# Convolutions that end in SiLU, and decay blocks made early, in a hybrid gMLP / gated DeltaNet / cross-attention layer

## The chip, the cores and the metric

The kernel runs on one core of a Trainium2 chip. The metric is device time in microseconds (us). The engines are named as the profile names them: PE is TensorE (matrix products), PEld its weight loads, DVE is VectorE, ACT is ScalarE, POOL is GpSimd, SP is SyncE, which issues most of the DMAs. Each engine works through its own instructions strictly in order; between engines there are semaphores.

## The reference, cut to what matters

One layer over 1024 tokens of width 2048: a norm, one input projection, three groups of heads, a gate on each, one output projection, a residual and a last norm. What the change touches is group B, a gated delta rule with 8 heads of width 128, in float32:

```python
def causal_conv_silu(x, w):                     # q, k and v of every head
    y = sum(w[k] * xp[:, k:k + S] for k in range(4))
    return jax.nn.silu(y)

qkv = causal_conv_silu(concat(d_q, d_k, d_v), conv_w)
q = l2norm(q) * 128 ** -0.5;  k = l2norm(k)
g = -exp(a_log) * softplus(d_a + dt_bias)       # log decay, one per token and head
g_cum = cumsum(g)                               # within a chunk
decay = exp(where(tri, g_cum[:, None] - g_cum[None, :], -inf))
a = where(strict, (k * beta) @ k.T * decay, 0)  # to be inverted, with 1 on the diagonal
attn_intra = where(tri, q @ k.T * decay, 0)
q_g = q * exp(g_cum)[:, None]
```

Two things of these are exponentials of the gate alone: the block `decay`, of which every pair of a chunk and a head has one, and the row factor `exp(g_cum)`, by which q is multiplied. Neither depends on q, k or v.

## The kernel before, in words

**Work and stages.** The sequence is taken in two halves of 512 tokens (`hf`), a half in four blocks of 128 (`NT`), and the kernel's delta rule takes chunks of 128 tokens (the reference has 64; the result is the same). A head's q, k and v are held with the 128 channels on the partitions and 512 tokens along the row. All large products run in three passes of split operands (`triple`, lines 460 to 464): a raw tile is cast on ScalarE to a high part (`whi`, `ahi`) and the rest is subtracted on VectorE (`wlo`, `alo`); `split_to` (437) does both. So every product of the projections hangs on ScalarE and VectorE.

The stages, with the times at which the profile has them:
- To about 124 us: the memory's keys and values, the norm of the first half of x, small parameters.
- The first stage, to about 413 us. For each half: the gate columns and `decays` (782), then the convolutions and preparation (`front`, 1128) of the first four heads, in two pairs, then their values (`early_values`, 1151). Results go to DRAM (`late_d`, `gt_d`). Weight tiles of 128 x 512 go through five buffers. Between these, `next_job` runs the norm of the second half of x and sums of row blocks that later products need.
- From about 413 us: the input projection's other columns, in five passes (`blocks(0)` to `blocks(4)`), each a seven-product scheme (`seven`, 1276). Beside them run the inverses (`inverse`, 971), the levels and scans of the first four heads (`backs`), then, at about 620 to 868 us, `front` for the last four heads, both halves, whose convolution inputs come back from DRAM (`p_d`), and later their values (`values`, 1175) and scans.
- From about 1280 us: the attention and the output projection.

**A convolution** (`conv`, 879). The projection's result is copied into `xr` with a halo of three tokens, ScalarE multiplies by the last of four weights, VectorE adds the other three (901). The weights in `cw` (672) are half of the given ones, so the sum is y/2. Lines 903 to 905 then make SiLU out of it: ScalarE takes tanh into a tile of the ring `tn`, and one VectorE instruction computes (t + 1) * y/2. There are 48 convolutions: q, k and v, eight heads, two halves; 24 in the first stage, 16 of q and k at 620 to 868 us, 8 of v later.

**A head's preparation** (`qk`, 915). GpSimd issues a DMA that spreads the head's cumulative decay over all partitions (`E`, 927; two buffers); ScalarE takes Exp of it for the row factor (`vs`, 929); then GpSimd masks E above the diagonal (930) and ScalarE takes Exp of each of its four blocks with a bias (933). E is scaled, multiplied into k k and q k products (953, 954), and q is multiplied by the row factor (955).

**Tables of ScalarE.** Functions come in tables; a change of table is an instruction of its own, ACT_TABLE_LOAD. SiLU, Exp and the tanh-GELU lie in different ones. Tanh, copies and squares need no change from the Exp table.

**Order of the work.** The program is first collected as a list of operations. `Plan.issue` (225) then simulates the engines with a price for each operation, and at every moment hands an engine, of the operations that are ready, the one of the lowest rank (`rank`, given where the operation is written; 5 if nothing is said). On ScalarE an operation that needs another table than the last one counts 1.5 ranks more (`STAY`, 253), and a load is priced at 1500 ns. `TABLES` (69) tells which functions this concerns: Exp, SiLU and GELU. The order found is what each engine then executes, and does not change at run time. Weight splits have rank 2, main products 9.

Of the kernel before, what the change touches and what calls it, by code (L numbers as in the profile page):

```python
# [17 lines left out]
P = 128  # L18
# [4 lines left out]
HT = 512  # L23
# [272 lines left out]
def kernel(  # L296
# [32 lines left out]
    def C(shape, name, dt=F32):  # L329
        return sb.tile(list(shape), dt, name=name, tag=name)[:]  # L330

    def DT(shape, name, dt=F32):
        return dr.tile(list(shape), dt, name=name, tag=name)[:]
# [41 lines left out]
    def tok(ap):  # L375

        return ap.rearrange("p (t c) -> p t c", c=P)
# [291 lines left out]
    pt = dnr()  # L669
    PE.transpose(pt[:, 0:105], rows[0:105], ident[0:105, 0:105])  # L670
    cw = C([P, 96], "cw")
    V.tensor_scalar(cw, pt[:, 0:96], 0.5, None, op0=ALU.mult)
    col2 = C([P, 9], "col2")
    V.tensor_copy(col2, pt[:, 96:105])

# [88 lines left out]


    abt = C([P, NT, 2 * NH], "abt")
    gr = C([NT * NH, P], "gr")
    y2 = C([P, 2 * NT, 64], "y2")
    G.memset(y2, 0.0)
    steps = C([P, HT], "steps")  # L770
    r3, ww = ([steps[:, i * P : (i + 1) * P] for i in two] for two in ((0, 1), (2, 3)))
    scs = [C([P, 7, NT, NH], f"sc{hf}") for hf in range(2)]
    sct = C([P, 5, NT, NH], "sct")
    gcs = [DT([NT, NH, P], f"gcd{hf}") for hf in range(2)]
    scan_banks, work = dnr.bufs[0:2], over(dnr.bufs[2:4])

    def decay_mm(a, k):
# [4 lines left out]
    def decays(hf, a):  # L782

        NU = NT * NH
        ab = ring["tn"]()[0:32]
        with rank(1):
            S.copy(ab, a[0:32])
        sc = scs[hf]
        beta, gg, gc, egl, edk, ngb, w0 = (sc[:, i] for i in range(7))
        w1, w2, w3, w4, egc = (sct[:, i] for i in range(5))  # L790
        tp = tpb()
        for tt in range(NT):
            PE.transpose(tp[:, tt * 32 : tt * 32 + 32], ab[:, tt * P : (tt + 1) * P], ident[0:32, 0:32])
        tpv = tp[:, 0 : NT * 32].rearrange("p (t c) -> p t c", c=32)
        with rank(1):
            S.copy(abt, tpv[:, :, 0 : 2 * NH])
            V.tensor_tensor(out=abt, in0=abt, in1=tpv[:, :, 2 * NH :], op=ALU.add)
            S.activation(beta, abt[:, :, NH:], AF.Tanh, scale=0.5)
            V.tensor_scalar(beta, beta, 1.0, 0.5, op0=ALU.add, op1=ALU.mult)
            V.tensor_tensor(out=w0, in0=abt[:, :, 0:NH], in1=rep(dtb, NT), op=ALU.add)  # L800
            S.activation(w1, w0, AF.Abs)
            S.activation(w1, w1, AF.Exp, scale=-1.0)
            V.tensor_scalar(w2, w1, 2.0, None, op0=ALU.add)
            V.reciprocal(w2, w2)
            V.tensor_tensor(out=w2, in0=w1, in1=w2, op=ALU.mult)
            V.tensor_tensor(out=w3, in0=w2, in1=w2, op=ALU.mult)
            V.tensor_scalar(w4, w3, 1.0 / 15.0, None, op0=ALU.mult)
            for c in (13.0, 11.0, 9.0, 7.0, 5.0, 3.0):
                V.scalar_tensor_tensor(w4, w4, 1.0 / c, w3, op0=ALU.add, op1=ALU.mult)
            V.scalar_tensor_tensor(w4, w4, 1.0, w2, op0=ALU.add, op1=ALU.mult)  # L810
            V.tensor_scalar(w0, w0, 0.0, None, op0=ALU.max)
            V.scalar_tensor_tensor(w0, w4, 2.0, w0, op0=ALU.mult, op1=ALU.add)
            V.tensor_tensor(out=gg, in0=w0, in1=rep(nal, NT), op=ALU.mult)
            dp = tpb()
            ggf = gg.rearrange("p t h -> p (t h)")
            PE.matmul(dp[:, 0:NU], utri, ggf, start=True, stop=True)
            PE.matmul(dp[:, NU : 2 * NU], ones, ggf, start=True, stop=True)
            gcf = gc.rearrange("p t h -> p (t h)")
            V.tensor_copy(gcf, dp[:, 0:NU])
            S.activation(egl.rearrange("p t h -> p (t h)"), dp[:, NU : 2 * NU], AF.Exp)  # L820
            V.tensor_tensor(out=edk.rearrange("p t h -> p (t h)"), in0=dp[:, NU : 2 * NU], in1=gcf,
                            op=ALU.subtract)
            S.activation(edk, edk, AF.Exp)
            S.activation(egc, gc, AF.Exp)
            V.tensor_scalar(ngb, egc, -1.0, None, op0=ALU.mult)
            V.tensor_scalar(w0, gc, -1.0, None, op0=ALU.mult)
            tp = tpb()
            PE.transpose(tp[0:NU, 0:P], gcf, ident)
            V.tensor_copy(gr, tp[0:NU, 0:P])
            Q.dma_start(gcs[hf].rearrange("t h p -> (t h) p"), gr)  # L830


    todo = []

# [44 lines left out]
    def conv(which, h, hf, o, a=None):  # L879
        ct = which * NH + h  # L880
        xr = ring["xr"]()
        w = [cw[:, k * 24 + ct : k * 24 + ct + 1] for k in range(4)]
        if h < NJ:
            if a is None:
                last = (which, h, hf) == (2, NJ - 1, 1)
                a = project([column(which, h)], order=(1, 0, 2, 3) if last else range(KT // KP))[0]
            next_job()
            with rank(1):
                S.copy(xr[:, 0:3], halo[:, which * NJ + h])
                S.copy(xr[:, 3:], a)  # L890
                if hf == 0:
                    S.copy(halo[:, which * NJ + h], xr[:, HT:])
                S.activation(o, xr[:, 3:], AF.Copy, scale=w[3])
        else:
            if hf == 0:
                G.memset(xr[:, 0:3], 0.0)
                Q.dma_start(xr[:, 3:], p_d[which][h - NJ][:, 0:HT])
            else:
                Q.dma_start(xr, p_d[which][h - NJ][:, HT - 3 :])
            S.activation(o, xr[:, 3:], AF.Copy, scale=w[3])  # L900
        for k in range(3):
            V.scalar_tensor_tensor(o, xr[:, k : k + HT], w[k], o, op0=ALU.mult, op1=ALU.add)
        t = ring["tn"]()
        S.activation(t, o, AF.Tanh)
        V.scalar_tensor_tensor(o, t, 1.0, o, op0=ALU.add, op1=ALU.mult)

    def by_token(o, src, scale):
        for tt in range(NT):
# [5 lines left out]

    def qk(h, hf, q, k, hs, gt):

        beta, edk, ngc = (scs[hf][:, i] for i in (0, 4, 6))
        bank = over(scan_banks) if h >= NJ else tpb
        qt, kt = to_tokens((q, bank()), (k, bank()))
        sumsq(hs[:, 1], kt)  # L920
        V.tensor_scalar(hs[:, 1], hs[:, 1], EPS, None, op0=ALU.add)
        V.reciprocal(hs[:, 3], hs[:, 1])
        V.scalar_tensor_tensor(hs[:, 2], hs[:, 3], -1.0, beta[:, :, h], op0=ALU.mult, op1=ALU.mult)
        V.tensor_tensor(out=hs[:, 3], in0=hs[:, 2], in1=edk[:, :, h], op=ALU.mult)
        kd = tok(ring["kd"]())
        e = tok(ring["E"]())
        G.dma_start(e, gcs[hf][:, h].partition_broadcast(P))
        vs = tok(ring["vs"]())
        S.activation(vs, e, AF.Exp)
        G.affine_select(out=e, in_=e, compare_op=ALU.is_ge, fill=NEG, base=0,  # L930
                        pattern=[[0, NT], [1, P]], channel_multiplier=-1)
        for tt in range(NT):
            S.activation(e[:, tt], e[:, tt], AF.Exp, bias=ngc[:, tt, h : h + 1])
        by_token(e, e, hs[:, 2])
        sumsq(hs[:, 0], qt)
        V.tensor_scalar(hs[:, 0], hs[:, 0], P * EPS, P * EPS * EPS, op0=ALU.mult, op1=ALU.add)
        by_token(kd, kt, hs[:, 3])
        rsqrt_to(hs[:, 4], hs[:, 1])
        V.tensor_tensor(out=hs[:, 4], in0=hs[:, 4], in1=hs[:, 1], op=ALU.mult)

        ch, cl = (ring["inv"](F32R).rearrange("p (t s c) -> p t s c", s=2, c=P) for _ in range(2))
        for i, src in enumerate((k, q)):
            split_to(ch[:, :, i], cl[:, :, i], tok(src), V)
        ai = tok(ring["ai"]())
        for t2 in range(NT // 2):
            d = work()
            for j in range(2):
                tt = 2 * t2 + j
                triple(d[:, j * 2 * P : (j + 1) * 2 * P], (ch[:, tt, 0], cl[:, tt, 0]), (ch[:, tt], cl[:, tt]),
                       True, True, R.cls)  # L950
            dv = d.rearrange("p (t s c) -> p t s c", s=2, c=P)
            ts = slice(2 * t2, 2 * t2 + 2)
            V.tensor_tensor(out=gt[:, ts], in0=dv[:, :, 0], in1=e[:, ts], op=ALU.mult)
            V.tensor_tensor(out=ai[:, ts], in0=dv[:, :, 1], in1=e[:, ts], op=ALU.mult)
        V.tensor_tensor(out=q, in0=q, in1=vs.rearrange("p t c -> p (t c)"), op=ALU.mult)
        return kd, ai, vs
# [237 lines left out]
    todo += [lambda i=i: prep1(i) for i in range(NT)]  # L1194
    todo += [lambda j=j: left_sums(j) for j in range(NJ)]
    gdrs = [front(0, 0, (first, None)), front(1, 0)]
    for h in range(NJ):
        early_values(h, 0)

# [14 lines left out]
    first = project([column(0, 0), column(1, 0)], before)  # L1214
    decays(1, a)
    gdrs += [front(0, 1, first), front(1, 1)]
    with rank(3):
        early_inv = inverse(gdrs, "early", 3)
    for h in range(NJ):
# [551 lines left out]
```

## Time and profile before

| | us |
|---|---|
| runs shown: median, lowest, highest | 1659.85, 1651.38, 1660.22 |
| the profiled execution | 1652.82 |
| its span, first to last instruction | 1651.1 |

The profile is of that one execution, and all durations below are from it. All of the program's instructions carry line 292, at which the planner emits them, so groups are told apart by the tiles that they write and read (`out<-in`), with buffer numbers left out: `E<-gcd` is the spread of the decays, `vs<-E` the row factor, `E<-E,sc` the decay Exps, `tn<-qT`, `tn<-kT` and `tn<-tn` the tanh passes of q, k and v. A group's line gives its count, its busy time in us, the mean ns of one, and how long its engine had idled before and what ended that.

The matrix products are pipelined; a product of 128 x 512 shows with some 390 ns, though the next one starts earlier. So a busy PE says that it never stood still, and its waits are read from the view of waits.

### The profile page before, as it was taken

The page shows a single profiled execution, that of the slowest core. Times are in us where ns is not written, and L with a number is a line of the kernel's source. Part 1 is how long each engine was busy: PE and PEld are TensorE (multiplying, and loading weights), DVE is VectorE, ACT ScalarE, POOL GpSimd, SP SyncE. Part 2 cuts the span into 40 slices and gives each one's busy share as a digit, 9 for nine tenths or more (in the row PEclk, how much of TensorE's full clock was granted, in tenths as well). Part 3 has the DMA queues.
Part 4 walks back from the last instruction along what each step waited for, and adds up shares of the span by engine and source line. Part 5 has one row for each costly group of instructions (what it writes and reads, how often), then busy time and mean ns, then how long its engine had stood idle before and what let it go on. Part 6 is the DMA issues. An engine that isn't in the chain of part 4 may idle for free.

```text
span 1651.1 us, 26126 instructions
## 1 busy us (share of the span) xinstructions
PE 1620.3 (98%) x8570; PEld 1356.5 (82%) x8570; DVE 1260.3 (76%) x2081; ACT 1033.7 (63%) x2226; POOL 296.8 (18%) x482
## 2 busy tenths in 40 slices
PE   8999999999999999999999999999999999999997
PEld 6878888887878888878878878888888888888886
DVE  4866877779755679889988877677768788789775
ACT  5957775765566548878665457666645785345345
POOL 0101310361442101322232153301000000000001
PEclk9999999999999999999999999999999999999999
DMA  7887898988976777689777897569778769688646
GB/s 248 258 235 216 242 297 258 256 263 291 369 256 212 277 252 253 203 279 335 265 255 242 280 281 265 193 223 375 254 273 267 242 208 337 233 261 303 226 143 239
DMA packets 278578, 427.89 MB, mean 259 GB/s; under 512 B 30829, under 2 KB 104102, under 8 KB 278442
## 3 DMA queue, kind: packets, MB, share of 16 engines
q1 hardware_dynamic: 255682, 365.76, 66.9%
q0 software_dynamic: 22144, 59.40, 11.5%
q8 instruction: 67, 1.10, 0.3%
q10 hardware_dynamic: 616, 1.07, 0.2%
q14 instruction: 69, 0.57, 0.1%
HBM read 338.52 MB, written 87.06 MB: 258 GB/s over the span
## 4 chain that ended last, share of the span: by engine, by line
PE 86%; DMA 7%; DVE 3%; issue 2%; ACT 2%; SPq 0%; POOL 0%; POOLq 0%; ACTq 0%; DVEq 0%
PE acc L292 66%; PE dn L292 20%; DMA wraw<-in_w_in_dram 2%; DMA raws<-sd 1%; DVE wlo L292 1%; DMA kT<-in_mem_dram 1%; DVE alo L292 1%; DMA y<-in_w_in_dram 1%; DMA ut<-in_x_dram 0%; ACT whi L292 0%; DMA ut<-udrearly 0%; DMA y<-sd 0%; DMA el<-vd 0%; DMA E<-in_gmlp_ws_dram 0%; DMA tblk<-tdrearly 0%
## 5 line engine op out<-in xcount | busy, mean ns | idle before, releaser
L292 PE MATMUL acc<-ahi,whi 128*128 128x512 f32 (+1 forms) x1152 | 451.6, 392 | 0.9 <-ACT whi L292 0.9
L292 PE MATMUL acc<-ahi,wlo 128*128 128x512 f32 (+1 forms) x1152 | 450.6, 391 | 0.1
L292 PE MATMUL acc<-alo,whi 128*128 128x512 f32 (+1 forms) x1152 | 450.2, 391 | 0.0
L292 PEld LDWEIGHTS acc<-ahi,whi 128*128 128x128 f32 x1152 | 216.9, 188 | 43.0 <-ACT whi L292 1.3
L292 PEld LDWEIGHTS acc<-ahi,wlo 128*128 128x128 f32 x1152 | 217.1, 188 | 42.0 <-DVE wlo L292 0.5
L292 PEld LDWEIGHTS acc<-alo,whi 128*128 128x128 f32 x1152 | 217.0, 188 | 40.9
L292 PE MATMUL acc<-ahi,zh 128*128 128x512 f32 x736 | 235.9, 396 | 0.0
L292 ACT CAST whi<-wraw 128x512 fp32r<-128x512 f32 (+1 forms) x170 | 137.0, 808 | 108.8 <-PE acc L292 77.6
L292 DVE TENSOR_TENSOR wlo<-wraw,whi 128x512 fp32r<-128x512 f32 (+1 forms) x170 | 156.9, 923 | 56.6 <-ACT whi L292 55.3
L292 DVE TENSOR_TENSOR alo<-raws,ahi 128x1024 fp32r<-128x1024 f32 x131 | 159.5, 1219 | 37.3 <-ACT ahi L292 36.5
L292 ACT CAST ahi<-raws 128x1024 fp32r<-128x1024 f32 x131 | 137.3, 1048 | 54.2 <-PE dn L292 29.3
L292 PEld LDWEIGHTS acc<-ahi,zh 128*128 128x128 f32 x736 | 138.0, 189 | 27.2
L292 PE MATMUL acc<-ahi,zl 128*128 128x512 f32 x368 | 145.2, 394 | 0.0
L292 POOL TENSOR_TENSOR small<-small,mhalf 128x1 f32<-128x1 f32 x26 | 16.8, 654 | 626.9 <-DVE small L292 626.8
L292 ACT CAST ahi<-y 128x1024 fp32r<-128x1024 f32 x65 | 68.2, 1050 | 37.9 <-PE acc L292 13.1
L292 DVE TENSOR_TENSOR ahi<-y,ahi 128x1024 fp32r<-128x1024 f32 x65 | 79.2, 1219 | 12.6 <-ACT ahi L292 12.4
L292 PEld LDWEIGHTS acc<-ahi,zl 128*128 128x128 f32 x368 | 69.5, 189 | 13.3
L292 DVE TENSOR_TENSOR wlo<-y,whi 128x1024 fp32r<-128x1024 f32 x34 | 41.5, 1221 | 24.7 <-ACT whi L292 22.4
L292 PE MATMUL dn<-wlo,ahi 128*128 128x512 f32 x152 | 59.0, 389 | 0.0
L292 PE MATMUL dn<-whi,alo 128*128 128x512 f32 x152 | 59.0, 389 | 0.0
L292 PE MATMUL dn<-whi,ahi 128*128 128x512 f32 x152 | 58.8, 389 | 0.0
L292 POOL TENSOR_TENSOR hs<-hs,mhalf 128x4 f32<-128x4 f32 x32 | 45.5, 1422 | 71.8 <-DVE hs L292 71.1
(410 smaller groups left out, 3293.8 us busy)
## 6 DMA issues: line engine op xcount, KB each, us to landing
wraw<-in_w_in_dram SPq DMA_DIRECT2D x268, 256.0 KB, 3.8
raws<-sd SPq DMA_DIRECT2D x148, 256.0 KB, 4.2
y<-in_w_in_dram SPq DMA_DIRECT2D x92, 256.0 KB, 4.9
y<-sd SPq DMA_DIRECT2D x77, 256.0 KB, 4.7
wraw<-in_w_out_dram SPq DMA_DIRECT2D x64, 256.0 KB, 4.1
raws<-h0d SPq DMA_DIRECT2D x54, 256.0 KB, 5.5
y<-in_w_out_dram SPq DMA_DIRECT2D x33, 256.0 KB, 4.6
sd<-zg SPq DMA_DIRECT2D x32, 256.0 KB, 4.1
```

Of the source, the lines that this page charges most:

```text
L292: o.fn(*o.args, **o.kw)
```

## The change

Three things.

- The convolution weights are kept as they are, and a convolution ends in one SiLU on ScalarE, in place. The tanh tile and the VectorE product fall away.
- The making of a decay block (spread, mask, four Exps) becomes a function. Heads 0 to 3 call it where the code stood. For heads 4 to 7 it is called in the first stage, once for each half, at rank 7, and the block is written to DRAM (`e_d`); their preparation later reads it back.
- `decays` also takes Exp of the 32 rows of cumulative decay (`egr`) and writes them to DRAM (`egs`); the row factor of every head is then a spread read from there, and no longer an Exp of E.

```diff
-    V.tensor_scalar(cw, pt[:, 0:96], 0.5, None, op0=ALU.mult)
+    V.tensor_copy(cw, pt[:, 0:96])
...
             Q.dma_start(gcs[hf].rearrange("t h p -> (t h) p"), gr)
+            S.activation(egr, gr, AF.Exp)
+            Q.dma_start(egs[hf].rearrange("t h p -> (t h) p"), egr)
+
+    def decay_block(hf, h, e):
+        G.dma_start(e, gcs[hf][:, h].partition_broadcast(P))
+        G.affine_select(out=e, in_=e, compare_op=ALU.is_ge, fill=NEG, base=0,
+                        pattern=[[0, NT], [1, P]], channel_multiplier=-1)
+        for tt in range(NT):
+            S.activation(e[:, tt], e[:, tt], AF.Exp, bias=scs[hf][:, 6, tt, h : h + 1])
+
+    def decay_blocks(hf, heads):
+        for h in heads:
+            e = tok(ring["E"]())
+            decay_block(hf, h, e)
+            G.dma_start(tok(e_d[hf][h]), e)
...
-        t = ring["tn"]()
-        S.activation(t, o, AF.Tanh)
-        V.scalar_tensor_tensor(o, t, 1.0, o, op0=ALU.add, op1=ALU.mult)
+        S.activation(o, o, AF.Silu)
...
         e = tok(ring["E"]())
-        G.dma_start(e, gcs[hf][:, h].partition_broadcast(P))
+        if h < NJ:
+            decay_block(hf, h, e)
+        else:
+            G.dma_start(e, tok(e_d[hf][h]))
         vs = tok(ring["vs"]())
-        S.activation(vs, e, AF.Exp)
-        G.affine_select(out=e, in_=e, compare_op=ALU.is_ge, fill=NEG, base=0,
-                        pattern=[[0, NT], [1, P]], channel_multiplier=-1)
-        for tt in range(NT):
-            S.activation(e[:, tt], e[:, tt], AF.Exp, bias=ngc[:, tt, h : h + 1])
+        G.dma_start(vs, egs[hf][:, h].partition_broadcast(P))
...
     gdrs = [front(0, 0, (first, None)), front(1, 0)]
+    with rank(7):
+        decay_blocks(0, range(NJ, NH))
...
     gdrs += [front(0, 1, first), front(1, 1)]
+    with rank(7):
+        decay_blocks(1, range(NJ, NH))
```

The planner orders the whole program anew, so instructions far from these lines can also change places.

More of the change, by code (lines that the diff above doesn't have):

```diff
@@ L766 @@
     abt = C([P, NT, 2 * NH], "abt")
-    gr = C([NT * NH, P], "gr")
+    gr, egr = (C([NT * NH, P], n) for n in ("gr", "egr"))
     y2 = C([P, 2 * NT, 64], "y2")
@@ L773 @@
     sct = C([P, 5, NT, NH], "sct")
-    gcs = [DT([NT, NH, P], f"gcd{hf}") for hf in range(2)]
+    gcs, egs = ([DT([NT, NH, P], f"{n}{hf}") for hf in range(2)] for n in ("gcd", "egd"))
+    e_d = [[DT([P, HT], f"ed{hf}_{h}") for h in range(NH)] for hf in range(2)]
     scan_banks, work = dnr.bufs[0:2], over(dnr.bufs[2:4])
@@ L915, in qk @@
     def qk(h, hf, q, k, hs, gt):
-        beta, edk, ngc = (scs[hf][:, i] for i in (0, 4, 6))
+        beta, edk = (scs[hf][:, i] for i in (0, 4))
         bank = over(scan_banks) if h >= NJ else tpb
```

## The prediction

> **What bounds the kernel now.** I read the page of the profiled execution first (busy shares, the chain), then the stretches of the span, then what TensorE waits for, then single groups. The page says who is full:
>
> ```profile
> span 1651.1 us, 26126 instructions
> PE 1620.3 (98%) x8570; PEld 1356.5 (82%) x8570; DVE 1260.3 (76%) x2081; ACT 1033.7 (63%) x2226; POOL 296.8 (18%) x482
> ...
> PE 86%; DMA 7%; DVE 3%; issue 2%; ACT 2%; SPq 0%; POOL 0%; POOLq 0%; ACTq 0%; DVEq 0%
> ```
>
> TensorE holds 86% of the chain that ended last and is busy for 98% of the span. The change has no TensorE instruction in it, so nothing of these 1620.3 us goes away; it can win only time in which TensorE stands still, and lose where it makes TensorE stand. The stretches say where that is. Columns: length, then PE, PEld, DVE, ACT and POOL busy with their counts, the clock, the DMA share, GB/s.
>
> ```profile
> 124.00:165.00 41.00, 41.00 (x207) 34.36 (x206) 25.51 (x47) 31.46 (x88) 6.72 (x9) 1.00 0.76 216
> ...
> sum 289.00, PE 288.02 PEld 239.44 DVE 222.41 ACT 193.56 POOL 80.09; mean PE 41.15 PEld 34.21 DVE 31.77 ACT 27.65 POOL 11.44
> ...
> 413.00:620.00 207.00, 203.85 (x1375) 172.83 (x1374) 132.15 (x203) 116.36 (x276) 58.23 (x102) 1.00 0.79 273
> 620.00:868.00 248.00, 242.79 (x1134) 201.80 (x1133) 219.45 (x354) 193.78 (x433) 68.81 (x102) 0.99 0.80 265
> ...
> 950.00:1115.00 165.00, 161.69 (x1181) 138.01 (x1180) 119.57 (x193) 108.89 (x256) 53.00 (x94) 1.00 0.74 241
> ```
>
> The sum row is that of 124 to 413 us, the first stage, in seven slices whose first stands above. In it TensorE is short of full by 1 us only. 620 to 868 us is the stage in which the last four heads are convolved and prepared: TensorE lacks 5.2 us there, VectorE is at 88% and ScalarE at 78%. What TensorE waited for, in us, times and longest, for 372 to 413, 413 to 620, 620 to 868 and 868 to 1640 us (124 to 372 has no wait at all):
>
> ```profile
> PE acc L292 <- ACT whi L292: 0.9, 1, 0.9
> ...
> PE dn L292 <- DMA ut<-udrearly: 1.5, 1, 1.5
> PE dn L292 <- issue: 1.2, 1, 1.2
> PE dn L292 <- ACT vs L292: 0.4, 1, 0.4
> ...
> PE dn L292 <- DVE inv L292: 2.6, 1, 2.6
> PE dn L292 <- ACT kd L292: 2.3, 1, 2.3
> PE dn L292 <- DVE ai L292: 0.3, 1, 0.3
> ...
> PE dn L292 <- DMA el<-vd: 2.5, 2, 2.1
> PE dn L292 <- ACT vs L292: 0.8, 1, 0.8
> ```
>
> They add up to 12.5 us. That is the whole prize, 0.8% of the time. The rest of the 30.8 us in which TensorE is not busy (1651.1 - 1620.3) lies before 124 us and after 1640 us, which the change does not reach.
>
> **The change part by part.** *Convolutions.* Each of the 48 loses one VectorE product and keeps one ScalarE pass; the tanh pass becomes a SiLU pass. The VectorE groups that go, the ScalarE passes that change, and the gates' SiLU and GELU passes of equal shape:
>
> ```profile
> L292 DVE SCALAR_TENSOR_TENSOR kT<-tn,kT 128x512 f32<-128x512 f32 x16 | 11.4, 712 | 1.8 <-ACT tn L292 1.8
> L292 DVE SCALAR_TENSOR_TENSOR qT<-tn,qT 128x512 f32<-128x512 f32 x16 | 11.3, 706 | 1.8 <-ACT tn L292 1.8
> L292 DVE SCALAR_TENSOR_TENSOR tn<-tn,tn 128x512 f32<-128x512 f32 x16 | 11.0, 688 | 3.6 <-ACT tn L292 3.5
> ...
> L292 ACT ACTIVATE tn<-qT 128x512 f32<-128x512 f32 x16 | 10.1, 629 | 1.5 <-DVE qT L292 1.4
> ...
> L292 ACT ACTIVATE y<-y 128x512 f32<-128x512 f32 x40 | 24.8, 633 | 4.5 <-DVE y L292 4.1
> ```
>
> VectorE loses 11.4 + 11.3 + 11.0 = 33.7 us; ScalarE's passes cost the same (629 against 633 ns). VectorE is not what TensorE waits for in the first stage, so what falls there is worth nothing to the end.
>
> *Tables.* Tanh shares a table with Exp, as the absence of loads before 641 us shows; SiLU does not. A load as the ScalarE timeline has it (start, us), then loads and Exp groups of 620 to 868 us, then the Exp groups of 124 to 413 us (which holds no load):
>
> ```profile
> 641.13 0.19 ACT L292 ACTIVATION_READ_ACCUMULATOR jk<-dn 128x1 f32 x1
> 641.34 1.28 ACT L292 ACT_TABLE_LOAD   x1
> 642.63 1.15 ACT L292 ACTIVATE y<-y 128x512 f32<-128x512 f32 x2
> ...
> L292 ACT ACT_TABLE_LOAD x6 | 7.7, 1283 | 0.1
> L292 ACT ACTIVATE E<-E,sc 128x128 f32<-128x128 f32 x32 | 10.6, 394 | 0.3 <-POOL E L292 0.3
> L292 ACT ACTIVATE vs<-E 128x512 f32<-128x512 f32 x8 | 5.0, 626 | 1.9 <-DMA E<-gcd 1.8
> ...
> L292 ACT ACTIVATE E<-E,sc 128x128 f32<-128x128 f32 x32 | 10.8, 395 | 0.0
> ```
>
> In 620 to 868 us the late heads then need no Exp at all: of six loads one is left. ScalarE there loses 5 x 1.28 = 6.4, 5.0 of row factors and 10.6 of decay Exps, 22.0 us of 193.8; VectorE loses 17 of the products above, at some 0.68 us about 11.5.
>
> In the first stage loads appear. By the code it has 24 SiLUs and 16 blocks of four Exps (8 of its own heads, 8 moved in); if each block falls between two SiLUs that is 32 loads, with two for each half's gate arithmetic 36; if blocks go in pairs, as the two E buffers and the planner's penalty on switching (STAY) allow, 16. I take the middle, 26. A load takes 1.28 us and stands between its neighbours with some 30 ns, so 1.31 each: 34 us. With 10.8 us of moved-in Exps (eight blocks cost what the eight there cost) and 5.0 us of row factors gone, ScalarE takes on 39.8 us: 193.6 becomes 233 of 289 us, 81%.
>
> The Trainium skill, "ScalarE: Activation LUTs", section "What ACT_TABLE_LOAD costs", gives a switch 1283 ns for the load and about 1380 ns more for a drain, 2.66 us; its 1283 agrees with this trace, the drain does not show in it. By that figure the 26 loads would be an estimated 69 us in place of 34.
>
> Does TensorE notice? What ScalarE waited for in 124 to 413 us:
>
> ```profile
> ACT whi L292 <- PE acc L292: 34.8, 45, 2.3
> ```
>
> 45 times the cast of the next weights stood ready and waited for TensorE to release a buffer. So the split weights run ahead by as many buffers as there are, and ScalarE has 34.8 us on that path alone before TensorE could be late. Casts are rank 2, SiLUs and Exps 5, moved-in blocks 7: a cast is held up by the one operation under way and a load before it. Bounds: 0 (all inside the 34.8), and 39.8 - 34.8 = +5 if every added microsecond ran ahead of a cast, +18 with 36 loads (52.9). I take +1, near the lower, because no wait exists there now.
>
> *The late stage.* Two of TensorE's waits can be followed back in the timelines of ScalarE and TensorE (brackets: idle before, and what ended it):
>
> ```profile
> 725.35 1.28 ACT L292 ACT_TABLE_LOAD   x1
> 726.64 0.63 ACT L292 ACTIVATE vs<-E 128x512 f32<-128x512 f32 x1
> ...
> 729.76 1.27 ACT L292 ACTIVATE E<-E,sc 128x128 f32<-128x128 f32 x4
> ...
> 731.94 0.58 PE L292 MATMUL dn<-inv,inv 128*128 128x256 f32 x1 [2.58 <-DVE inv L292]
> ...
> 834.83 0.72 ACT L292 ACTIVATE tn<-xr,cw 128x512 f32<-128x512 f32 x1 [4.08 <-DMA xr<-pd]
> ```
>
> The wait for the split of q into the inv tile comes just behind a load, a row-factor Exp and four decay Exps; all of them leave. That is -2.6. The wait for kd, 2.3 us, comes some 3 us after ScalarE stood 4.08 us for a convolution's input from DRAM, and that input stays. Bounds: 0, as other work may move into the freed place, and -5.2, all three. I take -2.6.
>
> *Row factors and kept blocks.* Sixteen spread reads from DRAM replace sixteen Exps; eight stores and eight plain loads are new; the sixteen spread reads of cumulative decay and their masks stay, eight of each earlier. All are issued by GpSimd. Issue ns on POOL, then KB and us to landing:
>
> ```profile
> L292 POOL TENSOR_SCALAR_AFFINE_SELECT E<-E 128x512 f32<-128x512 f32 x16 | 14.8, 924 | 34.9 <-ACT vs L292 34.8
> L292 POOL DMA_DIRECT2D E<-gcd x16 | 12.5, 783 | 22.6 <-DMA gcd<-gr 8.8 <-ACT tn L292 7.3 <-ACT jk L292 5.6
> L292 POOL DMA_DIRECT2D late<-ai x16 | 8.9, 558 | 29.2 <-ACT y L292 10.5 <-DVE ai L292 8.7 <-ACT jk L292 5.5
> ...
> E<-gcd POOLq DMA_DIRECT2D x16, 256.0 KB, 7.9
> ```
>
> POOL takes on 16 x 0.783 + 16 x 0.558 = 21.5 us on 296.8, where it is at 18%. The masks lose a wait: 34.8 us of POOL idling was for the Exp that read E before the mask overwrote it. The row factor now lands with E, in about 7.9 us, and is needed only by the last product of the head, behind the E products; I take 0. If it came late, VectorE would stand and weight splits queue behind it. A store must wait for four Exps and holds POOL's later transfers, those of the inverse's blocks among them; TensorE would then wait as it waits for the udrearly transfer (1.5 us). Bounds -1.5 (POOL's transfers come earlier without the idling) to +9 (the 7.9 us transfer once, and one 1.5 us wait doubled by it); I take 0, since 413 to 620 us has weight products to fill in. Traffic: 32 x 256 KB = 8.4 MB, of which 24 transfers (6.3 MB) fall on 289 us, 22 GB/s beside the 216 of the first slice; the stretch from 413 to 620 us carries 273 at a DMA share of 0.79 and waits for one transfer in it, so 0, and 1.5 us more at worst.
>
> *Small things.* Copying the convolution weights unscaled costs the same instruction; two Exps of 32 rows and two SP stores run once per half behind the decay arithmetic; in 950 to 1115 us two more loads (2.6 us) go where ScalarE idles 56 us. All 0.
>
> Sum: +1 - 2.6 + 0 = -1.6, rounded to -2. The profiled execution took 1652.82 (span and 1.7 around it). The median shown is 1659.85, 7.0 above it, and its neighbours are 1651.38 and 1660.22, so the four executions lie in two places with middle 1656. I set the -2 against that middle: 1654.
>
> **The rivals.**
> - *The waits go more widely.* The two loaded engines of 620 to 868 us lose 22.0 and 11.5 us, and every wait that rests on a late ScalarE or VectorE falls: 2.6 + 2.3 + 0.3 + 0.4 + 0.8 + 0.9 = 7.3, with shorter POOL idling the 2.7 us of udrearly and issue too: -10, 1646. For it: seven of nine waits are of these engines or POOL. Against: each is a single event, and an order laid out anew brings others.
> - *Slower: the loads reach TensorE.* Place: 124 to 413 us. It decides when the added ScalarE work ahead of casts passes the 34.8 us, from about 22 loads if all of it lies there, otherwise where one slice of 41 us takes on more than the 9.5 us that the first slice leaves (7 loads). Price by the same sum: +5 with 26 loads, +18 with 36, and +13 with 32 (41.9 + 5.8 - 34.8), which I take: 1669. Against: the casts' rank, and no wait now.
> - *A switch costs twice its load.* 26 x 1.28 us more, so 73 us added against 34.8: +38, 1694. Against: the load in the timeline ends at 642.62 and the next pass starts at 642.63. The Trainium skill's drain, cited above, would have this happen, and this trace does not bear it out.
> - *Slower by a store that blocks POOL:* +9, 1665, as above.
> - *Nothing comes of it*, because TensorE never waited for these engines: 1656, inside the forecast.
>
> **How the numbers follow.** Half a percent, 8.3 us, is about what a measurement here can tell. Forecast, with nothing coming of it, 0.45 (own range 1649 to 1662); wider gain 0.28; loads 0.18; store 0.07; double switch 0.02. So faster 0.28, same 0.45, slower 0.18 + 0.07 + 0.02 = 0.27. The double switch is the one case left outside the range. Low: the lower execution, 1651.38, less all 12.5 us of waits: 1639, say 1638. High: 1656 + 18: 1674.
>
> **What would show it.** After: no VectorE product behind a convolution's SiLU; some 16 to 36 loads before 413 us and one in 620 to 868; TensorE still at 41.0 of 41 in the slices of the first stage; the 2.6 us wait for inv gone. The forecast is wrong if TensorE's waits in 124 to 413 us exceed 5 us, or if waits of new places after 413 us add up to more than the 12.5 of now.

## The result and the profile after

| | before | after |
|---|---|---|
| median of 9 runs each, us | 1652.3 | 1665.44 |
| lowest to highest, us | 1649.45 to 1660.22 | 1659.96 to 1668.06 |
| ratio after / before | | 1.0075 [1.0056, 1.0094] |
| profiled execution, us | 1652.82 | 1665.44 |

The change makes the kernel slower by 0.75%, 12.4 us by the ratio (the medians lie 13.1 us apart); the forecast was 2 us faster. From the page of the kernel after:

```profile
span 1663.4 us, 26118 instructions
...
PE 1624.8 (98%) x8570; PEld 1359.7 (82%) x8570; DVE 1228.2 (74%) x2033; ACT 1055.3 (63%) x2239; POOL 307.8 (19%) x514
...
DMA packets 281233, 436.31 MB, mean 262 GB/s; under 512 B 31373, under 2 KB 104710, under 8 KB 281098
...
PE 79%; DMA 10%; DVE 4%; issue 3%; ACT 3%; POOL 0%; SPq 0%; POOLq 0%; DVEq 0%; ACTq 0%
```

VectorE lost 32.1 us (1260.3 before), as it should, and TensorE has the same 8570 products. But DMA holds 10% of the chain that ended last where it held 7%, and TensorE 79% instead of 86%: what stood between TensorE's products now are transfers. The groups of ScalarE after, each shape apart, show that the arithmetic was priced rightly:

```profile
L292 ACT ACT_TABLE_LOAD x43 | 55.2, 1283 | 4.6 <-DMA y<-in_mem_norm_g_dram 3.9
...
L292 ACT ACTIVATE kT<-kT 128x512 f32<-128x512 f32 x16 | 10.1, 629 | 5.8 <-DVE kT L292 5.7
```

A SiLU pass takes 629 ns, what the tanh pass took. The stretches after (columns as in the prediction: length, busy PE, PEld, DVE, ACT, POOL, clock, DMA share, GB/s):

```profile
124.00:165.00 41.00, 36.70 (x179) 30.90 (x180) 26.05 (x48) 35.68 (x92) 8.95 (x12) 0.92 0.79 227
...
372.00:413.00 41.00, 35.59 (x155) 28.96 (x153) 28.07 (x54) 24.77 (x52) 18.72 (x32) 0.92 0.96 301
...
sum 289.00, PE 277.59 PEld 229.59 DVE 194.08 ACT 220.84 POOL 95.30; mean PE 39.66 PEld 32.80 DVE 27.73 ACT 31.55 POOL 13.61
...
413.00:620.00 207.00, 204.18 (x1332) 172.53 (x1331) 136.76 (x216) 116.34 (x258) 57.51 (x103) 0.98 0.82 278
620.00:868.00 248.00, 243.49 (x1188) 203.79 (x1187) 214.83 (x353) 180.04 (x417) 59.29 (x95) 1.00 0.84 277
```

The first stage, where TensorE was short of full by 1 us, is now short by 11.4, nearly all in its first and its last slice, and in both the mean clock is 0.92. ScalarE is not what is full: 220.84 us there, less than the 233 of the forecast. What TensorE waited for after, in 112 to 131, 372 to 413, 413 to 620, 620 to 868 and 868 to 1645 us:

```profile
PE dn L292 <- DVE ut L292: 5.4, 1, 5.4
...
PE acc L292 <- ACT whi L292: 5.4, 1, 5.4
...
PE dn L292 <- DMA ut<-udrearly: 2.4, 1, 2.4
...
PE dn L292 <- DVE ai L292: 3.3, 2, 2.9
PE dn L292 <- DVE inv L292: 1.2, 1, 1.2
...
PE dn L292 <- ACT vs L292: 2.8, 1, 2.8
```

Two single waits of 5.4 us stand where before had 1.7 and 0.9. With four small ones (1.7 in all, 131 to 372 us) and 0.4 of issue, the waits are 22.6 us; before they were 14.2. The other part of the loss is in the clock. Four stretches of after, then two of before:

```profile
126.00:132.50 6.50, 4.20 (x14) 3.62 (x15) 6.30 (x12) 5.80 (x17) 2.91 (x4) 0.50 0.58 170
399.00:405.70 6.70, 4.11 (x10) 3.28 (x11) 6.55 (x10) 6.68 (x16) 2.53 (x4) 0.50 1.02 344
474.10:480.80 6.70, 6.60 (x62) 5.48 (x62) 4.23 (x6) 2.64 (x7) 2.26 (x5) 0.50 1.06 342
993.00:996.30 3.30, 3.10 (x9) 2.67 (x10) 3.30 (x6) 3.22 (x11) 0.00 (x0) 0.50 0.92 273
```

```profile
126.00:132.50 6.50, 6.50 (x35) 5.39 (x34) 4.45 (x7) 4.79 (x12) 0.00 (x0) 1.00 0.99 281
...
732.00:735.30 3.30, 3.30 (x10) 2.83 (x11) 3.30 (x4) 0.00 (x0) 0.00 (x0) 0.50 0.95 353
```

Each such stretch begins within a wait of TensorE or shortly behind it and lasts 3.41 or 6.83 us; in it a product of 128 x 512 follows the last one after 427 ns instead of 227. Before had two of 3.41 us (at the waits of 2.58 and 2.3 us), after three of 6.83 (at those of 5.4, 5.4 and 2.4) and one of 3.41 (at that of 2.8). That is 17.1 us more at half clock, so up to 8.5 us lost. With the 8.4 us of added waits this is an estimated upper bound of 17 for the 12.3 us by which the span grew. The Trainium skill, "TensorE: Matmul & The Clock Gate", Part 1, states a window of 3413 ns that runs freely and half rate after an idle window; the length of 3.41 us agrees, and so does a window that doesn't follow the program: the wait of 2.9 us at 711 us brought no half clock, that of 2.4 at 471 us did. The page's rule of no gaps over some 3.4 us is not enough here, since gaps of 2.3 to 2.8 us sufficed.

The traces of all 17 kernels show what lies behind that. Within each trace, these stretches begin on one grid of 3.413 us, to within 4 ns. Taken cell by cell (27 to 1640 us, cells at full clock), each of the 43 cells in which TensorE stood idle for 1.87 us or more was followed by half clock; of the 50 with 1.2 to 1.83 us, eight were. So it counts how much of a wait falls into one cell. The wait of 2.4 us at 471 us left 2.3 in one cell; that of 2.9 at 711 us was split into 1.1 and 1.8 (after; length, busy PE, clock, DMA share, GB/s):

```profile
470.64:474.05 3.41, 1.13 (x7) 1.00 1.06 330
709.57:712.98 3.41, 2.30 (x11) 1.00 0.91 289
712.99:716.40 3.41, 1.65 (x10) 1.00 0.67 231
```

Why the eight shorter ones had it, and why one stretch at 559 us and one at 33 us of z1 (a kernel of the experiments) came after cells with less than 0.8 us, stays open.

**The first place, 110 to 128 us.** All transfers issued in 104 to 126 us, before and then after (packets, MB and share of GpSimd's queue; then issues, KB each, median us to landing):

```profile
q0 software_dynamic: 160, 0.52, 12.5%
...
wraw<-in_w_in_dram SPq DMA_DIRECT2D x7, 256.0 KB, 5.2
...
E<-gcd POOLq DMA_DIRECT2D x2, 256.0 KB, 7.8
```

```profile
q0 software_dynamic: 538, 1.78, 34.3%
...
wraw<-in_w_in_dram SPq DMA_DIRECT2D x4, 256.0 KB, 11.9
...
vs<-egd POOLq DMA_DIRECT2D x4, 256.0 KB, 11.5
E<-gcd POOLq DMA_DIRECT2D x2, 256.0 KB, 8.8
```

GpSimd's queue takes 34.3% of the engines instead of 12.5%. The medians for weight tiles rest on few: the profile has the landing of two of the seven before (7.7 and 2.8 us) and of one of the four after (11.9). The timelines of GpSimd, ScalarE and TensorE after, and ScalarE's before:

```profile
110.35 1.69 POOL L292 DMA_DIRECT2D E<-gcd  x2 [5.42 <-ACT tn L292]
112.32 1.49 POOL L292 DMA_DIRECT2D vs<-egd  x2 [0.28 <-DMA egd<-egr]
...
115.42 1.49 POOL L292 DMA_DIRECT2D vs<-egd  x2
...
122.71 0.63 ACT L292 ACTIVATE jk<-ut 128x512 bf16<-128x512 f32 x1 [5.89 <-DMA ut<-in_x_dram]
...
125.24 0.63 ACT L292 ACTIVATE jk<-ut 128x512 bf16<-128x512 f32 x1 [1.80 <-DMA ut<-in_x_dram]
...
128.30 1.11 PE L292 MATMUL dn<-ident,ut 128*128 128x128 f32 x4 [5.44 <-DVE ut L292]
```

```profile
120.40 0.63 ACT L292 ACTIVATE jk<-ut 128x512 bf16<-128x512 f32 x1 [2.54 <-DMA ut<-in_x_dram]
```

Before, the row factors were computed from E, so only two spread reads were under way. Now the four `vs` buffers are free, nothing else holds their reads back, and six spread reads of 256 KB start within 6 us, just when the norm of the second half needs its tiles of x. ScalarE stands 5.89 us for one of them, and TensorE 5.44 us for the transposes of the normed rows. Before, the wait at this place was 1.7 us.

**The second place, 377 to 402 us.** The issues of the input tiles of the next stage (`raws`), before and then after, and GpSimd, SP's queue, ScalarE and TensorE after:

```profile
raws<-h0d SPq DMA_DIRECT2D x8, 256.0 KB, 3.5
```

```profile
raws<-h0d SPq DMA_DIRECT2D x8, 256.0 KB, 8.0
```

```profile
376.91 0.78 POOL L292 DMA_DIRECT2D E<-gcd  x1
...
387.27 0.76 POOL L292 DMA_DIRECT2D E<-gcd  x1
...
387.36 1.85 SPq L292 DMA_DIRECT2D raws<-h0d  x4
...
395.94 1.05 ACT L292 CAST ahi<-raws 128x1024 fp32r<-128x1024 f32 x1 [3.38 <-DMA raws<-h0d]
...
400.49 1.05 ACT L292 CAST whi<-wraw 128x1024 fp32r<-128x1024 f32 x1
...
401.59 0.80 PE L292 MATMUL acc<-ahi,whi 128*128 128x512 f32 x1 [5.41 <-ACT whi L292]
```

The kept blocks of the second half, at rank 7, are pushed to the end of the stage, where the input tiles of the next stage are loaded. The medians rest on three known landings before and on one after. These tiles are issued at 387.4 us (379.8 before) and reach ScalarE at 395.9; ScalarE, in order, stands for them, the weight cast behind them comes at 400.49, and TensorE waits for it.

### The profile page after: what moved, and what is told of

Its sections match the earlier page's. It is cut to its first block, busy times and chain, and to the rows that moved or that the text cites. A ratio compares the mean times of both kernels' runs of the same rounds, so it can differ in the third digit from the quotient of the medians.

```text
span 1663.4 us, 26118 instructions
## 1 busy us (share of the span) xinstructions
PE 1624.8 (98%) x8570; PEld 1359.7 (82%) x8570; DVE 1228.2 (74%) x2033; ACT 1055.3 (63%) x2239; POOL 307.8 (19%) x514
## 4 chain that ended last, share of the span: by engine, by line
PE 79%; DMA 10%; DVE 4%; issue 3%; ACT 3%; POOL 0%; SPq 0%; POOLq 0%; DVEq 0%; ACTq 0%
PE acc L292 59%; PE dn L292 20%; DMA wraw<-in_w_in_dram 2%; DMA y<-in_w_in_dram 1%; DMA wraw<-hTd 1%; DMA hTd<-tn 1%; ACT whi L292 1%; DVE wlo L292 1%; DMA raws<-sd 1%; DMA raws<-h0d 1%; DMA kT<-in_mem_dram 1%; ACT E L292 0%; DVE qT L292 0%; DMA vs<-od 0%; DMA y<-sd 0%
## 5 line engine op out<-in xcount | busy, mean ns | idle before, releaser
L292 PEld LDWEIGHTS acc<-ahi,zl 128*128 128x128 f32 x368 | 69.2, 188 | 13.1
L292 ACT CAST zh<-wraw 128x1024 fp32r<-128x1024 f32 x36 | 37.8, 1050 | 39.2 <-PE acc L292 17.2
L292 ACT ACT_TABLE_LOAD x43 | 55.2, 1283 | 4.6 <-DMA y<-in_mem_norm_g_dram 3.9
```

The lines of the kernel that those rows point to most:

```text
L292: o.fn(*o.args, **o.kw)
```

## The experiments

Three theories, with the letters that the expectations use. A: the added transfers crowd out loads that TensorE's input hangs on, the row-factor reads at the first place and the kept blocks at the second. B: the table loads hold ScalarE up and so TensorE. C: the new order as such, whatever is in it. In the first set the order of after is kept exactly and one operation in it does something else, so that nothing but that operation's cost moves. "Net" is the ratio less 1 times 1652.3, in us; `ut` and `whi` are TensorE's waits at the two places, of one profile each. A difference of two nets is known to some 4 to 5 us either way, as estimated from the two intervals.

| run | ratio to before | net | ut | whi |
|---|---|---|---|---|
| after | 1.0075 [1.0056, 1.0094] | +12.4 | 5.4 | 5.4 |
| x1_rowset | 1.0003 [0.9985, 1.0022] | +0.5 | 2.8 | 6.0 |
| x2_blockset | 1.0055 [1.0034, 1.0076] | +9.1 | 5.5 | 1.6 |
| x3_bothset | 0.9955 [0.9940, 0.9971] | -7.4 | 3.3 | 1.6 |
| x5_tanhset | 1.0037 [1.0015, 1.0059] | +6.1 | 5.6 | 5.8 |
| x6_plainread | 1.0061 [1.0034, 1.0089] | +10.1 | 6.6 | 7.2 |
| x7_allset | 0.9977 [0.9953, 1.0001] | -3.8 | 2.8 | 1.6 |
| x4_silu | 1.0028 [1.0011, 1.0046] | +4.6 | 2.8 | 1.5 |
| z4_rowread | 1.0095 [1.0067, 1.0124] | +15.7 | 8.8 | 0.9 |
| z5_blocks | 1.0041 [1.0021, 1.0061] | +6.8 | none | 6.7 |
| z1_earlyexp | 1.0097 [1.0063, 1.0131] | +16.0 | 3.3 | 6.3 |
| z2_earlyexp_later | 1.0058 [1.0039, 1.0076] | +9.6 | 3.1 | 1.4 |
| w1_gated | 1.0118 [1.0069, 1.0167] | +19.5 | 5.2 | 7.7 |
| w2_gated_later | 1.0111 [1.0073, 1.0150] | +18.3 | 2.6 | 0.9 |
| w3_gated_bothlater | 1.0101 [1.0071, 1.0130] | +16.7 | 3.3 | 0.9 |
| v1_blocks_later | 1.0021 [1.0000, 1.0042] | +3.5 | none | 0.9 |

### The transfers, in the order of after

x1: the sixteen row-factor reads become fills on the same engine.

```diff
         G.dma_start(vs, egs[hf][:, h].partition_broadcast(P))
+        R.ops[-1].fn = lambda out, src: nc.gpsimd.memset(out, 1.0)
```

> The changed kernel with every instruction in the same order, but the 16 spread reads of row factors are replaced, at the same place on GpSimd, by a memset of the row factor to 1 (q is then not scaled; the transfers alone are left out). Theory A, that the spread reads which become ready together at about 112 us crowd out the rows of x that TensorE's next transposes need: TensorE's wait for ut (5.4 us) falls to the 1.8 us of the kernel before or less, and the run is some 4 to 6 us faster than the changed kernel, about 1660. Theory B, that the table loads on ScalarE make the loss: the wait stays at some 5 us and the time at 1665.

x2: the four spread reads of the second half's kept blocks become fills; the Exps and the stores stay.

```diff
+            n = len(R.ops)
             decay_block(hf, h, e)
+            if hf == 1:
+                R.ops[n].fn = lambda out, src: nc.gpsimd.memset(out, NEG)
```

> The changed kernel in the same order, but the four spread reads that fetch the cumulative decay for the kept blocks of the second half are replaced, at the same place on GpSimd, by a memset (those four blocks come out as zero). Theory A, that these transfers, issued as the first stage ends, hold up the loads of the first operands of the next stage: TensorE's wait for whi at about 396 us (5.4 us) falls to 1 to 3 us, time about 1662. Theory B (table loads) and theory C (the new order on ScalarE, which puts other work ahead of that cast): the wait stays above 4.5 us and the time at 1665.

x3 makes both edits.

> Both replacements in one, again in the same order. Theory A: the two gains add, 1656 to 1659, so that little is left of the loss of 13 us. Theories B and C: 1663 to 1665, the loss stays.

TensorE's waits at the two places, x1 and then x2:

```profile
PE dn L292 <- DVE ut L292: 2.8, 1, 2.8
...
PE acc L292 <- ACT whi L292: 6.0, 1, 6.0
```

```profile
PE dn L292 <- DVE ut L292: 5.5, 1, 5.5
...
PE acc L292 <- ACT whi L292: 1.6, 1, 1.6
```

Each edit shortens the wait of its own place and leaves the other within 0.6 us. The row reads are worth 11.9 us (12.4 to 0.5). The four reads of the second place are worth 3.3 alone, which is not clear of the noise, and 7.9 once the row reads are gone (x1 to x3), which is. Both together give 19.8, and without both the kernel is faster than before. That 19.8 is more than the sum may be chance, or part of what is gained at one place is waited out at the next; no run tells these apart. At the second place the link is plain: in x2 the tiles `raws`, issued at 388.6 us, land in 3.9 us instead of 8.0, and ScalarE waits 0.06 us for them instead of 3.38.

The first place explains the smaller part of the row reads' 11.9 us: its wait falls by 2.6 us and its time at half clock from 6.83 to 3.41 us, so at most some 4.3 us. And 2.8 us of that wait stay in x1, and in x4 below, which has none of the added transfers; x7 below, which has no table load there either, keeps 2.8 too, so the step from 1.7 to 2.8 us belongs to the new order. The rest of the 11.9 us lies later. x1 and x3 have no wait of TensorE in 620 to 868 us, where before had 5.2 and after has 4.5; so the gain that the forecast sought there can be had, in a kernel whose row factors cost nothing.

### The table loads, in the order of after

x5: the instruction that is planned as SiLU is executed as tanh, so one table serves nearly all, and 11 loads are left of 43.

```diff
         S.activation(o, o, AF.Silu)
+        R.ops[-1].fn = lambda out, src, f: nc.scalar.activation(out, src, AF.Tanh)
```

> The changed kernel in the same order on every engine, but each convolution's SiLU pass is executed as a tanh pass of the same length (the values are then not the SiLU of the sum). Tanh lies in the table of Exp, so some 32 of the 43 table loads fall away and nothing else changes. It prices the loads alone. Theory A (spread reads): the waits for ut at 122 us (5.4 us) and for whi at 396 us (5.4 us) stay within 1 us, and the time falls by 3 us at most, to 1662 or more. Theory B (loads): both waits shrink and the time falls by 8 us or more.

```profile
PE dn L292 <- DVE ut L292: 5.6, 1, 5.6
...
PE acc L292 <- ACT whi L292: 5.8, 1, 5.8
```

The two waits (the same view, x5) stay as they are, so theory B doesn't explain them. But 6.3 us went (1.5 to 11 with its noise), between the two expectations: the loads do cost something in that order. What went are the small waits of the first stage and parts of two later ones: the wait for the udrearly transfer is 0.7 us instead of 2.4, that for vs after 868 us 0.2 instead of 2.8. x7 then puts x3 and x5 together.

> The changed kernel in the same order, with all three taken away: row factors set to 1 on GpSimd, the second half's kept blocks set and not read, and the tanh pass in place of SiLU, so that no table load is added. If these three make the loss and the rest of the change is worth what the run without the first two showed: 1641 to 1646, below the 1648.65 of that run by some of the 6 us that the loads cost alone. If the loads cost only where the transfers already made TensorE late: 1647 to 1650.

x7 (1648.56 us) and x3 (1648.65) have the same time. Against the kernel before of its own set, x7 is even 3.6 us the slower of the two, within the noise. With the transfers away, taking out 32 table loads gains nothing that can be measured: in this order they cost time only together with the transfers.

### Is it the bytes, or the spreading?

x6: each row read becomes a load of 256 KB whose rows lie apart in DRAM (128 rows of 2 KB) instead of one row read 128 times.

```diff
         G.dma_start(vs, egs[hf][:, h].partition_broadcast(P))
+        R.ops[-1].fn = lambda out, src: nc.gpsimd.dma_start(out, tok(x[0:P, 0:HT]))
```

> The changed kernel in the same order, with each of the 16 spread reads replaced by a plain load of equal size (256 KB) in rows of 2 KB of the input x, which is then used as the row factor (the values are not the row factors). If the spread reads cost by their bytes: 1663 to 1667, with TensorE's wait for ut near 5 us. If they cost by their short packets of 512 bytes: 1656 to 1661, the wait at 3 to 4 us, towards the 1655.8 of the run without the reads.

Issues in 104 to 126 us, x6:

```profile
wraw<-in_w_in_dram SPq DMA_DIRECT2D x5, 256.0 KB, 9.2
...
vs<-in_x_dram POOLq DMA_DIRECT2D x4, 256.0 KB, 10.2
```

At the first place the spreading is not what costs: the loads land in 10.2 us (11.5 spread), the wait of TensorE is 6.6 us, and the total is the same within the intervals. The packets do not differ either: the trace has both kinds as 64 packets of 4096 bytes for each transfer, not as the 512 bytes that the expectation named. In 620 to 868 us x6 shows no wait of TensorE, where after has 4.5 us; there the spreading may matter, or chance, with one profile of each.

### Each part alone, on the kernel before

Here the planner lays out a new order each time. x4 has the SiLU alone (the diff of the change, lines 672 and 903 to 905), z4 the row factors alone, z5 the kept blocks alone, with tanh and the row factors by Exp.

> The kernel before with the first part of the change alone: convolutions end in one SiLU, decay blocks and row factors are made as before (the planner orders anew). Over 25 table loads in the first stage and more than the six in 620 to 868 us, no added transfer. Theory A: no new wait at 122 or 390 us, within 4 us of the kernel before. Theory B: slower by 8 us or more, with TensorE waiting for casts between 124 and 413 us.

> The kernel before with the third part of the change alone: the row factors of all heads are spread reads of stored Exps; convolutions and decay blocks as before, so ScalarE has 10 us less and no new table load. Theory A (the spread reads crowd other transfers): slower by 5 to 11 us, with TensorE waiting 4 to 6 us for ut at about 122 us. Theory B (table loads make the loss): the same time as the kernel before, or faster by up to 3 us.

> The kernel before with the second part alone: decay blocks of the last four heads made in the first stage and kept, convolutions with tanh; row factors of the first four heads by Exp of E as before, of the last four by a spread read of the decays and an Exp. Theory A: slower by 2 to 7 us, with a wait for whi of 4 us or more where the first stage ends (about 390 us). Theory B: no change, for no table load is added.

TensorE's wait at the first place in z4, and at the second in z5:

```profile
PE dn L292 <- DVE ut L292: 8.8, 1, 8.8
```

```profile
PE acc L292 <- ACT whi L292: 6.7, 1, 6.7
```

Each part brings the wait that theory A gives to it and not the other's: row reads 8.8 us at the first place and 0.9 at the second, kept blocks none and 6.7. Every part alone is slower than before, and their ratios add up to 1.64% where all three together cost 0.75%: the costs don't add. x4 has 51 loads and none of the transfers. Its wait at the first place is 1.1 us longer than before, with 3.41 us at half clock behind it that before did not have; its other large waits lie after 620 us, for the inverse's operand `ai` from VectorE (5.0 and 2.8 us). Whether the loads or only the new order made these isn't settled by it. By size, the expectations were often off although the places were right: x1 gained more than forecast, x2 less, and z4 lost 15.7 us where 5 to 11 were expected.

### Attempts to keep the gain

z1 takes the first four heads' row factors by Exp of E again, z2 also puts the second half's kept blocks behind the second product of the next stage. w1 holds the row reads back until the head's q and k are turned to tokens, w2 adds z2's delay, w3 delays the blocks of both halves. v1 is z5 with the second half's blocks delayed.

```diff
+        turned = R.ops[-1]                        # w1, w2, w3
...
-        G.dma_start(vs, egs[hf][:, h].partition_broadcast(P))
+        with behind(turned):
+            G.dma_start(vs, egs[hf][:, h].partition_broadcast(P))
...
     blocks(0, to_conv(0), to_conv(1))
+    with rank(7), behind(ends[1, 3]):             # z2, w2, v1
+        decay_blocks(1, range(NJ, NH))
```

> The changed kernel, but the first four heads take their row factor by Exp of E again, as the kernel before did; the last four read it spread. So the reads that became ready together at about 112 us are gone, ScalarE has 5 us more and the order is made anew. Theory A: the wait for ut falls from 5.4 to 2 to 3 us, the wait at the end of the first stage stays near 5; 1657 to 1662. Theory B: 1665 or more, since ScalarE has more to do and the table loads stay.

> The same, and the kept blocks of the second half are made later: behind the second product of the next stage (about 455 us), out of the way of the first operands of that stage. Theory A: both waits are at 3 us or less, 1649 to 1656, at the kernel before or under it. Theory B: 1663 or more.

> The changed kernel with one dependency more: a head's spread read of its row factor is issued only when the transposes of its q and k are done, so four of them no longer start together at 112 us. Same bytes, same engine; the order is made anew. Theory A with the clock: the wait for ut falls below 3 us, that at the end of the first stage stays near 5 us; 1657 to 1662. If the loss is of the bytes and not of the moment, 1664 or more.

> The same, and the kept blocks of the second half are made behind the second product of the next stage (about 455 us). Theory A: neither wait is above 3 us; 1650 to 1657, near the kernel before. If the bytes count and not the moment: 1660 or more.

> The same, with the kept blocks of both halves made there, so that the first stage holds no transfer or Exp of them, and fewer table loads; the stretch from 480 to 560 us, in which the transfers of the kernel before stand at a share of 0.55 to 0.70, takes them. Theory A: 1648 to 1655, at or under the kernel before. If the bytes count and not the moment: as the run with one half moved.

> A correct version: the kept blocks alone, with tanh convolutions and row factors by Exp for the first four heads, and the second half's blocks made behind the second product of the next stage. Against the run with the kept blocks alone (1661) the wait for whi as the first stage ends falls from 6.7 to 1 to 2 us, and half clock behind it goes: 1651 to 1656. If a new order brings as much elsewhere, as it did with the gated reads: 1659 or more.

None beats the kernel before, and none reached what theory A expected of it. Five (all but v1, which fell between its two ranges) came out in the range of the other reading: table loads for z1 and z2, "the bytes count and not the moment" for w1 to w3. So that a read costs nothing at another moment is not shown for the whole time, only for the two waits. The whi wait is 5.4 to 7.7 us in all seven kernels that read the second half's decays at the stage's end (after, x1, x5, x6, z1, z5, w1) and 0.9 to 1.6 in the ten others, the kernel before among them. The ut wait is 5.4 to 8.8 in the five with four early row reads (after, x2, x5, x6, z4), and at most 3.3 in the nine with none. With one such read it is 5.2, 2.6 and 3.3 us (w1, w2, w3): here one trace differs from the next by as much as the reads add. And each new order brought waits at new places, v1 for example this one (413 to 620 us):

```profile
PE dn L292 <- DVE states L292: 5.9, 1, 5.9
```

So theory C holds beside A: an order laid out anew costs some microseconds in places that no local reading gave. Why each order gets the waits that it has stays open; there is one profile of each.

## Why the prediction was wrong, by its own steps

- **Convolutions.** Right: a SiLU pass costs the tanh pass (629 ns), VectorE lost 32.1 us (33.7 forecast), and no run prices that alone; x4, which has it together with the loads, was 4.6 us slower.
- **Tables.** The counts were right: 26 in 124 to 413 us, one in 620 to 868. The load stood alone at 1283 ns with no drain behind it, so the rival of the double switch is out. "I take +1, near the lower" was too low for this order: with 32 of 43 loads gone 6.3 us go (x5). But the path given to the rival "the loads reach TensorE" was not it: neither of the two great waits moved, and without the transfers the loads cost nothing that can be measured (x7 against x3).
- **The late stage.** Half right. The wait for inv fell from 2.6 to 1.2 us, but `ai` brought 3.3. With the row reads away the whole 5.2 us of waits there are gone (x1, x3), and with plain loads in their place too (x6), so that what the row reads do there is not settled by their bytes. In the kernel as it is, VectorE's wait for weight tiles in that stage rose from 2.4 to 9.3 us.
- **Row factors and kept blocks, and traffic: the step that failed.** It put both at 0 ("the row factor now lands with E, in about 7.9 us"; "so 0, and 1.5 us more at worst"). The runs give 11.9 us for the row reads, 3.3 alone (7.9 without the row reads) for four reads of kept blocks, 19.8 for both. Three things were wrong in it. I took the 24 transfers as spread evenly over 289 us, 22 GB/s more, and looked at who waits for *them*. But they come in bursts, where the order lets them start, and the cost falls on what else is under way at that moment: tiles of x at 115 us, `raws` at 387. And the DMA share of the stretch says nothing of such a moment: before shows 0.76 for 124 to 165 us, and 0.99 for 126 to 132.5 within it. Last, I counted TensorE's waits from 124 us on and wrote that what lies earlier is not reached; the wait for ut begins at 122 us, was 1.7 us long, and became 5.4. What the eight late row reads cost by, in 620 to 868 us, stays open.
- **The clock.** No term of the sum had it. A wait of TensorE was priced at its length; from some 2.3 us on it often cost up to 1.7 or 3.4 us more (estimated from half the clock for 3.41 or 6.83 us), depending on how it fell into the cells.
- **The base.** The -2 was set against 1656; the nine runs of the kernel before have the median 1652.3. This error of 3.7 us went against that of the sum and hid a part of it.
- **The rivals.** "A store that blocks POOL" named 1665 us, by luck: in the timeline of the second place the one store on which GpSimd stands long (`late<-vs`, 9.50 us) is not one of the kept blocks', and it waits for ScalarE, which stands behind `raws`. "Wider gain" (1646) comes near x3 and x7 (7.4 and 3.8 us faster than before, 10 named). Their row factors cost nothing, so it is a bound on what the change could have gained, not a gain that was there to take.
- **What would show it.** The stated sign of a failure, over 5 us of TensorE's waits in 124 to 413 us, came: 5.4 and 1.7 there, beside the 5.4 that straddles 124 us. Waits after 413 us add up to 10.1, under the 12.5 named.

## What to carry to other kernels

A new DMA is priced at the moment at which it will start, not by the mean share of its stage: ask which buffer is free, what then holds it back, and which load that TensorE's next operand hangs on is issued within the same few microseconds. Here four reads that waited for nothing but the stored rows started within 4 us of each other. Replacing Exps by reads of the results moved work from an engine with slack to transfers without (a DMA share of 0.96 in 112 to 128 and in 377 to 402 us, where before had 0.82 and 0.89). To price one cost of a program whose order a planner makes, keep the order and change what one operation executes: new orders here moved the time by more than several of the effects that were asked about.

## What the runs showed of the hardware that was not expected

- TensorE's half clock follows a fixed grid of 3.413 us: 1.87 us or more of standing still within one cell was followed by it in all of 43 cells, while waits of 2.9 and 3.3 us that two cells shared were followed by none (after at 711 us, z1 at 124 us).
- A spread read of 2 KB to 128 partitions and a load of 128 rows of 2 KB cost this kernel the same within the intervals (1.0075 and 1.0061); the trace has both as 64 packets of 4096 bytes, and they landed in 11.5 and 10.2 us.
- The cost of 32 table loads of 1283 ns was 6.3 us in one order and not measurable in the same order without 20 transfers (sixteen row reads and four reads of decays).
